# Input projection and gate: one 512-column matmul for both parts of the operand against the high weights, halves added on reading

## The chip, the core and the metric

The kernel runs on one core of one Trainium2 chip. A core has a matrix engine (PE, with its weight loads shown as PEld), a vector engine (DVE), a scalar engine (ACT), a general engine (POOL) and a queue engine (SP); each takes its instructions in order. PE writes to PSUM, which has eight banks; a bank holds 512 float32 numbers in each of the 128 partitions. The metric is the device time of one execution in microseconds (us): before the change the median of three runs is 992.47 us (992.36 to 992.50).

## The reference, cut to what matters

Two layers over 256 tokens of width 2048, all in float32:

```python
for i in range(DEPTH):                                  # DEPTH = 2
    u = _rmsnorm(h, norm_g[i]) @ w_in[i]                # input projection
    a_val, a_glu, a_z, q, k, v, b_z = jnp.split(u, offs, axis=-1)
    ya = _conformer_conv(a_val, a_glu, ...) * silu(a_z) # GLU, width-31 convolution, LayerNorm
    yb = _window_attention(q, k, v, bias_band, sink[i]) * silu(b_z)
    h = h + jnp.concatenate([ya, yb], axis=-1) @ w_out[i]   # output projection
    e = _rmsnorm(p[i] @ w_pe[i], pe_g[i])               # embedding
    h = h + e * sigmoid(h @ w_pg[i])                    # gate
return _rmsnorm(h, final_g)
```

## The kernel before, in words

**Products in parts.** Operands are kept transposed, channels in the partitions and the 256 tokens in the columns. To stay near float32 with a fast matmul type, each operand is the sum of a rounded high part and a low part (`hgh`, `hgl` for the normed input; `yah`/`yal`, `ybh`/`ybl` for the two branches; `h1h`, `h1l` for the residual), and so is each weight (`hi`, `lo`). A product of a 128x128 weight block with a 128x256 operand tile, called a *product* below, is three matmuls in `mm3` (lines 384 to 387): hi x high (L385), hi x low (L386), lo x high (L387). Each loads its own weights.

**Weight stream.** All weights come in 1 MB chunks in the order of use. Half a chunk (eight 128x128 blocks, a *half*) is split by `split` (L156 to L164): ACT casts it to `hi` (L161), then DVE subtracts to get `lo` (L164). `get(h)` is called at the start of the step that multiplies half h and splits up to half h+4 (there are five buffers, `NSPL`), so the parts run four halves ahead of PE.

**Stages of a layer.** The embedding `e`; then the input projection: eight convolution tiles `ag` (value and GLU column tile, a pair of output tiles in one PSUM bank), the keys `k`, the values `v` (other operand order, L580 to L582), four pairs each of `zb` and `q` in turn, and four pairs `za`; then the output projection `o`, and the gate `g`. A pair is four halves or 32 products. When a pair is complete, a consumer reads its bank: `glu` (ACT sigmoid L541, DVE multiply L542), casts and subtracts for the keys (L565, L567), SiLU on ACT for `zb` and `za` (L649, L669), scaling on ACT and DVE for `q` (L655, L656), sigmoid on ACT for `g` (L775).

**Side work.** After each step `pump` lets the side work go on: 2.6 to 3.3 taps of the convolution (L532, DVE; 240 taps a layer), and one step of attention, whose scores, transposes and values (`sc`, `pt`, `av`) each take PSUM banks for a while. At the end of the input projection DVE makes `ybl` (L713), which the output projection needs first.

**What sets the order.** PE, DVE and ACT carry out their instructions in the order in which the program text issues them, so an instruction that waits holds up everything behind it on its engine. The loads run on SP's queue and a few on POOL's. PSUM is one pool of eight banks, `ps`. The scratch tag `sq` has three buffers; one is held from the start by `oh` until the bias is prepared, during the `ag` stage.

Of the kernel before, what the change touches and what calls it, by code (L numbers as in the profile page):

```python
# [17 lines left out]
P = 128  # L18
# [42 lines left out]
# the convolution's column tiles, those that share the first operand's first half together  # L61
# [18 lines left out]
def weight_halves():  # L80
    """One layer's weights in the order of use: (matrix, columns, first k tile, k tiles)."""
# [39 lines left out]
# columns of the small per-channel parameters, one layer after the other  # L121
# [5 lines left out]
def trunk_kernel(ctx: ExitStack, tc: tile.TileContext, xT, pT, wst, par, gain, relb, sinkp, onehot, out):  # L127
# [4 lines left out]
    big = ctx.enter_context(tc.tile_pool(name="big", bufs=10))  # L132
# [4 lines left out]
    ps = ctx.enter_context(tc.tile_pool(name="ps", bufs=8, space=PSUM))  # L137
    dram = ctx.enter_context(tc.tile_pool(name="dram", bufs=1, space=DRAM))

    def bigt(name, dt=F32):  # L140
        return big.tile([P, 8, S], dt, tag="big", name=name)
# [15 lines left out]
    def split(h):  # L157
        raw = raws[h // 2][:, h % 2, :]
        hi = wspl.tile([P, HALF], F32R, tag="hi", name=f"hi{h}")
        lo = wspl.tile([P, HALF], F32R, tag="lo", name=f"lo{h}")  # L160
        nc.scalar.copy(hi, raw)  # L161
        spl[h] = (hi, lo)
        if h != 4:
            (nc.gpsimd if h in LOPOOL else nc.vector).tensor_sub(lo, raw, hi.bitcast(F32))  # L164

    def first_lo(x):
        """Half of the first half's low part."""
        s = slice(x * HALF // 2, (x + 1) * HALF // 2)
        nc.vector.tensor_sub(spl[4][1][:, s], raws[2][:, 0, s], spl[4][0][:, s].bitcast(F32))

    def ahead(h):
        """The parts of the halves up to h, and the loads that run ahead of them."""
# [9 lines left out]
    def get(h):  # L182
        """The two parts of half h."""
# [37 lines left out]
    def later(f, *args):  # L221
        """f(*args) with the next pump."""
# [11 lines left out]
    def finish(l):  # L234
        """What is left of the convolution and the attention."""
# [13 lines left out]
    # products of zeros while the first loads run, so that the PE's clock is up  # L249
    zeros = wk.tile([P, S], F32, name="zeros", tag="sq", bufs=3)  # L250
# [10 lines left out]
    def load_half(c, x, n=1):  # L261
        """Half of a chunk, in n parts."""
# [9 lines left out]
    h = [bigt(f"x{i}") for i in range(2)]  # L272
# [33 lines left out]
    oh = wk.tile([NUM_BUCKETS + 1, NREL], F32, name="oh", tag="sq", bufs=3)  # L306
# [5 lines left out]
    # keys, each head's parts twice, to meet the high and the low part of its queries  # L312
# [5 lines left out]
    def bias_prep():  # L318
# [3 lines left out]
        fs = wk.tile([NQ, NREL], F32, name="fs", tag="sq", bufs=3)  # L322
# [3 lines left out]
    def load_bias(i):  # L326
        """Minus the band's bias of tile i's two heads, [query, head, 3 * P - 1 - key of the band]."""
# [7 lines left out]
    def rstd_col(parts, dim, name, between=None):  # L335
        """(mean of squares + eps) ** -0.5 of each token, [P, 2]; parts: [P, S] partial sums."""
# [16 lines left out]
    def rstd_row(dg, name, tag="rb", copy=True):  # L353
        """The same in every row, [P, S]."""
# [16 lines left out]
    def square_acc(acc, src, first, eng=None):  # L371
        """acc += src * src, [P, 2, S]."""
# [3 lines left out]
        sq = wk.tile([P, 2, S], F32, name="sq", tag="sq", bufs=3)  # L376
# [7 lines left out]
    def mm3(o, wh, wl, xh, xl, start, stop):  # L384
        nc.tensor.matmul(o, wh, xh, start=start, stop=False, skip_group_check=True)  # L385
        nc.tensor.matmul(o, wh, xl, start=False, stop=False, skip_group_check=True)  # L386
        nc.tensor.matmul(o, wl, xh, start=False, stop=stop, skip_group_check=True)  # L387
# [4 lines left out]
    def step(o, X, start, stop):  # L392
        """The next half of the stream, times X, onto o."""
        steps([o], X, [start], stop)

    def steps(os, X, starts, stop):
        """The next halves of the stream (of the same rows), in turn by row tile."""
        parts = []
        for _ in os:
            name, _, k0, nk = HALVES[Cursor.h % NHALF]  # L400
            parts.append([a.rearrange("p (k c) -> p k c", k=nk) for a in get(Cursor.h)])
            Cursor.h += 1
        for kk in range(nk):
            k = k0 + kk
            for o, (hi, lo), start in zip(os, parts, starts):
                mm3(o, hi[:, kk, :], lo[:, kk, :], X[0][k // 8][:, k % 8, :], X[1][k // 8][:, k % 8, :],
                    start and kk == 0, stop and kk == nk - 1)
# [16 lines left out]
    for l in range(DEPTH):  # L424
        # ======== E: the layer's own embedding ========
        e = [bigt(f"e{l}_{i}") for i in range(2)]
        eacc = wk.tile([P, 2, S], F32, name="eacc", tag="hacc")
        # the first operand
        hg = ([], [])
        rbs, subs = [], []  # L430

        def operand(k, l=l, h=h, hg=hg):
            """Two tiles of the normed input, as parts."""
            i, kk = k // 8, k % 8
            if kk == 0:
                hg[0].append(bigt(f"hgh{l}_{i}", F32R))
                hg[1].append(bigt(f"hgl{l}_{i}", F32R))
# [458 lines left out]
```

## Time and profile before

| | |
|---|---|
| median of 3 runs | 992.47 us |
| the profiled execution: span | 992.5 us |
| PE busy | 972.7 us (98%), 7896 matmul records |
| DVE busy | 760.6 us (77%) |
| ACT busy | 545.6 us (55%) |
| POOL busy | 90.2 us (9%) |
| input projection, first layer | from 27.8 to 309.6 us |
| output projection, first layer | from 310.7 to 404.4 us |
| gate, first layer | from 404.4 to 496.7 us |
| second layer: input projection, gate | 512 to 790 us, 884.7 to 977 us |

The span of the profiled execution is its whole time; it stands at the median of the runs. Busy time says how long an engine had something in work, not that it was at its best pace: matmul records overlap, since the start of the next is what counts. In a timeline row the first number is the start, the second the length (of all, where several are merged), and what stands in brackets is the idle time of that engine just before, with the instruction that ended it.

### The profile page before, as it was taken

What the parts mean: (1) busy time and instruction counts of PE and PEld (TensorE: products, weight loads), DVE (VectorE), ACT (ScalarE), POOL (GpSimd) and SP (SyncE); (2) the same over time, 40 slices, a digit from 0 to 9 for tenths busy, and PEclk for the clock granted to TensorE, in tenths of its full rate; (3) what the DMA queues carried; (4) which work ended last, traced back from release to release, by engine and by line L of the source; (5) the groups of instructions that cost most, each with busy time, mean ns of one, the idle gap of its engine ahead of it and who ended that gap; (6) DMA issues with size and microseconds to landing.
All of it is one profiled execution on the core that took longest, in us unless ns stands there. A gap on an engine that the chain in (4) does not pass through costs nothing.

```text
span 992.5 us, 19137 instructions
## 1 busy us (share of the span) xinstructions
PE 972.7 (98%) x7896; PEld 952.6 (96%) x7896; DVE 760.6 (77%) x1284; ACT 545.6 (55%) x824; POOL 90.2 (9%) x91
## 2 busy tenths in 40 slices
PE   8999999999999999999999999999999999999994
PEld 6899999999999999999999999999999999999994
DVE  3899989987787666676658998988887867666653
ACT  4555454878774554444355444568777545445441
POOL 2113001001000000011103200000100000100110
PEclk9999999999999999999999999999999999999997
DMA  7665536555545466446556455455444435654522
GB/s 281 239 218 186 189 139 216 190 184 166 186 155 180 140 229 238 171 170 231 180 189 215 179 189 210 161 195 189 158 163 167 170 133 205 218 195 171 194 86 86
DMA packets 28888, 182.56 MB, mean 184 GB/s; under 512 B 3461, under 2 KB 4021, under 8 KB 8960
## 3 DMA queue, kind: packets, MB, share of 16 engines
q1 hardware_dynamic: 25200, 168.34, 47.2%
q0 software_dynamic: 3600, 12.99, 4.6%
q8 instruction: 62, 1.02, 0.4%
q14 instruction: 26, 0.21, 0.1%
HBM read 177.09 MB, written 4.23 MB: 183 GB/s over the span
## 4 chain that ended last, share of the span: by engine, by line
PE 94%; issue 3%; DVE 1%; POOL 1%; ACT 0%; POOLq 0%; DVEq 0%; ACTq 0%
PE o L385 6%; PE o L386 6%; PE o L387 6%; PE ag L386 6%; PE ag L385 6%; PE ag L387 6%; PE g L387 6%; PE g L386 6%; PE g L385 6%; PE za L385 3%; PE zb L385 3%; PE q L385 3%; PE zb L386 3%; PE q L386 3%; PE za L386 3%
## 5 line engine op out<-in xcount | busy, mean ns | idle before, releaser
L164 DVE TENSOR_TENSOR lo<-raw,hi 128x1024 fp32r<-128x1024 f32 x301 | 366.7, 1227 | 132.8 <-ACT hi L161 132.5
L161 ACT CAST hi<-raw 128x1024 fp32r<-128x1024 f32 x304 | 312.7, 1046 | 191.4 <-PE ag L386 46.0
L532 DVE SCALAR_TENSOR_TENSOR acc<-a,pars,acc 128x241 f32<-128x241 f32 (+11 forms) x480 | 217.8, 503 | 1.0
L386 PE MATMUL ag<-hgl,hi 128*128 128x256 f32 x512 | 145.1, 283 | 1.7 <-DVE hgl L445 1.7
L385 PE MATMUL ag<-hgh,hi 128*128 128x256 f32 x512 | 145.5, 284 | 0.0
L385 PE MATMUL g<-h1h,hi 128*128 128x256 f32 x512 | 144.9, 283 | 0.0
L386 PE MATMUL g<-h1l,hi 128*128 128x256 f32 x512 | 144.9, 283 | 0.0
L387 PE MATMUL g<-h1h,lo 128*128 128x256 f32 x512 | 144.9, 283 | 0.0
L387 PE MATMUL ag<-hgh,lo 128*128 128x256 f32 x512 | 144.9, 283 | 0.0
L386 PEld LDWEIGHTS ag<-hgl,hi 128*128 128x128 f32 x512 | 98.3, 192 | 2.2 <-DVE hgl L445 2.1
L385 PEld LDWEIGHTS ag<-hgh,hi 128*128 128x128 f32 x512 | 98.3, 192 | 1.2 <-ACT acc L525 0.8
L385 PEld LDWEIGHTS g<-h1h,hi 128*128 128x128 f32 x512 | 98.3, 192 | 0.0
L386 PEld LDWEIGHTS g<-h1l,hi 128*128 128x128 f32 x512 | 98.3, 192 | 0.0
L387 PEld LDWEIGHTS g<-h1h,lo 128*128 128x128 f32 x512 | 98.3, 192 | 0.0
L387 PEld LDWEIGHTS ag<-hgh,lo 128*128 128x128 f32 x512 | 98.3, 192 | 0.0
L385 PE MATMUL za<-hgh,hi 128*128 128x256 f32 x256 | 73.7, 288 | 0.0
L385 PE MATMUL o<-ybh,hi 128*128 128x256 f32 x256 | 73.3, 286 | 0.0
L385 PE MATMUL q<-hgh,hi 128*128 128x256 f32 x256 | 73.3, 286 | 0.0
L385 PE MATMUL zb<-hgh,hi 128*128 128x256 f32 x256 | 73.1, 286 | 0.0
L386 PE MATMUL o<-ybl,hi 128*128 128x256 f32 x256 | 72.5, 283 | 0.0
L385 PE MATMUL o<-yah,hi 128*128 128x256 f32 x256 | 72.4, 283 | 0.0
L386 PE MATMUL o<-yal,hi 128*128 128x256 f32 x256 | 72.4, 283 | 0.0
(214 smaller groups left out, 2277.9 us busy)
## 6 DMA issues: line engine op xcount, KB each, us to landing
raw<-in_wst SPq DMA_DIRECT2D x153, 1024.0 KB, 4.9
bias<-fscr POOLq DMA_DIRECT2D x16, 384.0 KB, 3.8
raw<-in_wst SPq DMA_DIRECT2D x5, 512.0 KB, 10.7
x<-in_xT SPq DMA_DIRECT2D x4, 512.0 KB, 11.4
hx<-in_xT POOLq DMA_DIRECT2D x8, 256.0 KB, 3.5
hscr<-e POOLq DMA_DIRECT2D x2, 1024.0 KB, 4.4
hx<-hscr POOLq DMA_DIRECT2D x8, 256.0 KB, 3.4
out_t<-og SPq DMA_DIRECT2D x7, 256.0 KB, 2.4
```

The source lines that it names most:

```text
L161: nc.scalar.copy(hi, raw)
L164: (nc.gpsimd if h in LOPOOL else nc.vector).tensor_sub(lo, raw, hi.bitcast(F32))
L385: nc.tensor.matmul(o, wh, xh, start=start, stop=False, skip_group_check=True)
L386: nc.tensor.matmul(o, wh, xl, start=False, stop=False, skip_group_check=True)
L387: nc.tensor.matmul(o, wl, xh, start=False, stop=stop, skip_group_check=True)
L532: nc.vector.scalar_tensor_tensor(acc[:, t, lo_:hi_], a[:, t, lo_ + s:hi_ + s], w(k), acc[:, t, lo_:hi_], ALU.mult, ALU.add)
```

## The change

The two parts of an operand now lie in one tile, `[P, 2, 8, S]`, so that high and low of a k tile can be read as one moving operand of 512 columns; the two parts of a weight half lie in one tile `w`. Where an output has a whole bank to itself, `mm3` issues two matmuls in place of three: the high weights against both parts at once (512 columns into the 512 of the bank), and the low weights against the high part onto the second half of the bank. An output tile then takes a bank instead of half a bank, and a pair takes two. On reading, `merge` adds the halves: ACT copies the second halves of the two banks to SBUF (`hl`, one buffer), DVE adds the first halves, and the consumers read the sum in SBUF. This is done for `ag`, `k`, `zb`, `q`, `za` and `g`; `o` and `v` keep three matmuls. PSUM is now two pools: `ps` with four single banks and `ps2` with two double ones. The tag `sq` goes from three buffers to two, the large tiles from ten to five of twice the size. Comments are dropped.

```diff
-    big = ctx.enter_context(tc.tile_pool(name="big", bufs=10))
+    big = ctx.enter_context(tc.tile_pool(name="big", bufs=5))
...
-    ps = ctx.enter_context(tc.tile_pool(name="ps", bufs=8, space=PSUM))
+    ps = ctx.enter_context(tc.tile_pool(name="ps", bufs=4, space=PSUM))
+    ps2 = ctx.enter_context(tc.tile_pool(name="ps2", bufs=2, space=PSUM))
...
+    def banks(name):
+        return ps2.tile([P, 2, 2, S], F32, tag="ps2", name=name)
...
-        sq = wk.tile([P, 2, S], F32, name="sq", tag="sq", bufs=3)
+        sq = wk.tile([P, 2, S], F32, name="sq", tag="sq", bufs=2)
...
-    def mm3(o, wh, wl, xh, xl, start, stop):
-        nc.tensor.matmul(o, wh, xh, start=start, stop=False, skip_group_check=True)
-        nc.tensor.matmul(o, wh, xl, start=False, stop=False, skip_group_check=True)
-        nc.tensor.matmul(o, wl, xh, start=False, stop=stop, skip_group_check=True)
+    def mm3(o, w, x, start, stop):
+        if len(o.shape) == 3:
+            nc.tensor.matmul(o, w[:, 0], x, start=start, stop=False, skip_group_check=True)
+            nc.tensor.matmul(o[:, 1], w[:, 1], x[:, 0], start=False, stop=stop, skip_group_check=True)
+            return
+        nc.tensor.matmul(o, w[:, 0], x[:, 0], start=start, stop=False, skip_group_check=True)
+        nc.tensor.matmul(o, w[:, 0], x[:, 1], start=False, stop=False, skip_group_check=True)
+        nc.tensor.matmul(o, w[:, 1], x[:, 0], start=False, stop=stop, skip_group_check=True)
+
+    def merge(b):
+        n = b.shape[1]
+        t = wk.tile([P, 2, S], F32, name="hl", tag="hl", bufs=1)[:, 0:n, :]
+        nc.scalar.copy(t, b[:, :, 1, :])
+        nc.vector.tensor_add(t, b[:, :, 0, :], t)
+        return t
...
     def pair(X, name):
-        b = bank(name)
+        b = banks(name)
         for x in range(2):
-            step(b[:, x, :], X, x == 0, False)
-            step(b[:, x, :], X, False, True)
-        return b
+            step(b[:, x], X, True, False)
+            step(b[:, x], X, False, True)
+        return merge(b)
...
         def glu(t, b):
+            b = merge(b)
             u = wk.tile([P, S], F32, name=f"u{l}_{t}", tag="sg")
             nc.scalar.activation(u, b[:, 1, :], AF.Sigmoid)
             nc.vector.tensor_mul(a[:, t, :], b[:, 0, :], u)
```

Where the prediction speaks of orders, these are the rows. On ACT, at the end of convolution tile 3 of the first layer (`sq<-e` are the embedding's squares, `u` the sigmoid of the GLU, `hi` or `w` the casts of the weights), before:

```order
L161 CAST hi_747<-raw_608 128x1024
L377 ACTIVATE sq<-e_0_130 128x512
L161 CAST hi_781<-raw_608 128x1024
L541 ACTIVATE u_3_812<-ag_3_676 128x256
L161 CAST hi_818<-raw_677 128x1024
```

and now:

```order
L170 CAST w_624<-raw_518 128x1024
L386 ACTIVATE sq<-e_132 128x512
L170 CAST w_649<-raw_518 128x1024
L408 COPY hl<-ag_3_571 128x512
L562 ACTIVATE u_3_674<-hl 128x256
L170 CAST w_680<-raw_572 128x1024
```

The copy of `merge` is new, and the sigmoid behind it now reads what DVE has added; the next cast stands behind both. On DVE at the same place, before:

```order
L532 SCALAR_TENSOR_TENSOR acc_266<-a_265,pars,acc_266 128x251
L532 SCALAR_TENSOR_TENSOR acc_266<-a_265,pars,acc_266 128x253
L532 SCALAR_TENSOR_TENSOR acc_266<-a_265,pars,acc_266 128x252
L542 TENSOR_TENSOR a_265<-ag_3_676,u_3_812 128x256
L164 TENSOR_TENSOR lo_819<-raw_677,hi_818 128x1024
```

and now:

```order
L552 SCALAR_TENSOR_TENSOR ac_261<-ac_261,pars 128x251
L552 SCALAR_TENSOR_TENSOR ac_261<-ac_261,pars 128x253
L552 SCALAR_TENSOR_TENSOR ac_261<-ac_261,pars 128x252
L409 TENSOR_TENSOR hl<-ag_3_571,hl 128x512
L563 TENSOR_TENSOR ac_261<-hl,u_3_674 128x256
L173 TENSOR_TENSOR w_680<-raw_572,w_680 128x1024
```

The add stands behind the taps of the last step, and ahead of the GLU's multiply and the next low part. For `zb` and `za` there is no multiply: the low part follows the add directly.

More of the change, by code (lines that the diff above doesn't have):

```diff
@@ L270, in load_x @@
         nc.sync.dma_start(h[k // 8][:, k % 8:k % 8 + 4, :], xT[:, k:k + 4, :])
-    h = [bigt(f"x{i}") for i in range(2)]
+    h = halves(bigt("x"))
     pf = load_p(0)
@@ L545, in trunk_kernel @@
         for ts in FIRST_TILES:
-            bs = [bank(f"ag{l}_{t}") for t in ts]
+            bs = [banks(f"ag{l}_{t}") for t in ts]
             for n in range(2):
@@ L716, in trunk_kernel @@
         side.append(lgen)
-        Y = ([ya[0], yb[0]], [ya[1], yb[1]])
-        ob = [bank(f"o{l}_{j}") for j in range(NB_FIRST // 2)]
+        Y = [ya, yb]
+        ob = []
+        for j in range(2):
+            b = banks(f"o{l}_{j}")
+            ob += [b[:, 0], b[:, 1]]
+        ob += [bank(f"o{l}_{j}") for j in range(4, NB_FIRST // 2)]
         for j in range(NB_FIRST):
@@ L804, in trunk_kernel @@
         for j in range(KT - 2, KT):
-            b = bank(f"g{l}_{j}")[:, 0:1, :]
-            step(b[:, 0, :], h1, True, False)
-            step(b[:, 0, :], h1, False, True)
-            gate(j, b)
+            b = banks(f"g{l}_{j}")[:, 0:1]
+            step(b[:, 0], h1, True, False)
+            step(b[:, 0], h1, False, True)
+            gate(j, merge(b))
         drain()
```

89 lines of the change are left out of this document (41 added, 48 removed).

## The prediction

> **What bounds the kernel now.** I read the page first, then the chain of waits, then stretches of the input projection, then single rows there.
>
> ```profile
> PE 972.7 (98%) x7896; PEld 952.6 (96%) x7896; DVE 760.6 (77%) x1284; ACT 545.6 (55%) x824; POOL 90.2 (9%) x91
> PE 94%; issue 3%; DVE 1%; POOL 1%; ACT 0%; POOLq 0%; DVEq 0%; ACTq 0%
> ```
>
> PE carries 94% of the chain, and nothing else holds it for long: the bound is the pace of its matmuls. That pace is read from starts, not lengths. From the timeline of PE and its loads, and the chain:
>
> ```profile
> 850.25 0.28 PE L385 MATMUL o<-yah,hi 128*128 128x256 f32 x1
> 850.25 0.19 PEld L386 LDWEIGHTS o<-yal,hi 128*128 128x128 f32 x1
> 850.37 0.28 PE L386 MATMUL o<-yal,hi 128*128 128x256 f32 x1
> 496.68 5.18 PE e L462 x24
> L385 PE MATMUL g<-h1h,hi 128*128 128x256 f32 x512 | 144.9, 283 | 0.0
> ```
>
> A 256-column matmul follows the one before by 120 ns, so a product of three takes 360 ns. The load for the next matmul begins with the matmul it hides under. The float32 matmuls of the embedding, whose two records stand for four passes over 256 columns, take 5.18/24 = 216 ns a record, 108 per 256 columns: longer streams seem to carry less surplus than 120 ns, and the surplus looks like the weight load.
>
> But the 77% of DVE is a mean. These are stretches of the two input projections, between a low part that DVE makes at the end of a tile and another (first layer: end of tile 1, end of the first `q` pair, start of `ybl`; second layer alike), and the two gates; after PE and PEld comes DVE:
>
> ```profile
> 54.72:174.76 120.04, 120.04 (x994) 119.00 (x993) 114.40 (x192) 58.85 (x77) 18.59 (x14) 1.00 0.55 192
> 174.76:308.99 134.23, 134.23 (x1113) 128.92 (x1113) 112.97 (x250) 98.71 (x184) 9.11 (x11) 1.00 0.52 177
> 536.61:655.20 118.59, 118.59 (x989) 118.54 (x989) 112.34 (x191) 57.20 (x74) 14.34 (x9) 1.00 0.53 187
> 655.20:789.20 134.00, 134.00 (x1111) 128.71 (x1111) 112.41 (x250) 98.44 (x184) 7.10 (x8) 1.00 0.48 169
> 404.40:496.70 92.30, 92.30 (x771) 92.30 (x770) 61.11 (x75) 41.21 (x48) 8.32 (x7) 1.00 0.55 193
> 884.70:977.00 92.30, 92.30 (x773) 92.30 (x771) 56.95 (x73) 45.33 (x61) 7.75 (x6) 1.00 0.39 138
> ```
>
> In the first half of a projection DVE works 95% of the time, and there it runs behind PE. The sigmoid on ACT marks the end of a tile on PE, the next row of DVE the low part that follows:
>
> ```profile
> 66.03 0.38 ACT L541 ACTIVATE u<-ag 128x256 f32<-128x256 f32 x1 [1.95 <-PE ag L387]
> 67.39 1.23 DVE L164 TENSOR_TENSOR lo<-raw,hi 128x1024 fp32r<-128x1024 f32 x1
> 77.56 0.38 ACT L541 ACTIVATE u<-ag 128x256 f32<-128x256 f32 x1 [1.95 <-PE ag L387]
> 79.45 1.21 DVE L164 TENSOR_TENSOR lo<-raw,hi 128x1024 fp32r<-128x1024 f32 x1
> ```
>
> DVE needs 12.06 us for a tile that PE does in 11.53. So PE and DVE are level in that half; in the gates DVE has a third to spare.
>
> **The change part by part.** *PE, the pace.* Removed: one of three matmuls and loads in each of 1856 products (`ag`, `g` 512 each; `zb`, `q`, `za` 256 each; `k` 64). What 512 columns of this type cost is not in the trace. From below: two streams without surplus, 216 + 108 = 324 ns. From above: 120 ns for every 256 columns, 360, no gain. I take 216 + 120 = 336: the low weights load under the long matmul, the next high weights under the short one, which stays load-bound. That is 24 ns a product, 0.77 us a pair, 44.5 us in all if nothing else binds.
>
> The Trainium skill ("TensorE: Matmul & The Clock Gate", Back-to-back issue gap) gives N/2.4 + 2.5 ns between isolated warm matmuls, 109 for 256 columns and 216 for 512. The embedding's rows agree with the second, the 120 ns disagree with the first; by the rule alone only 2.5 ns a product would be won, 1.3 us in the gates, and the sum below would come to 1008 (the rival without gain in pace, to within 2 us).
>
> *Gates.* DVE and ACT have room for the merges there: the added copy, add and repeated wait take some 2 us of a pair of 10.8, and the parts run four halves ahead. So 512 products x 24 ns = **-12.3 us**, between -18.4 and 0.
>
> *Input projections.* Here each `merge` adds an ACT copy and a DVE add, and, as the orders show, a loop: DVE adds, ACT reads the sum, ACT then casts the next weights, DVE then makes their low part. Before, ACT read PSUM as soon as PE was done, and its casts were ready when a late DVE came to them. Now a late DVE finds ACT blocked behind its own add, and waits out the loop. The prices:
>
> ```profile
> L741 DVE TENSOR_TENSOR hx<-o,hx 128x512 f32<-128x512 f32 x16 | 11.0, 691 | 7.5 <-PE o L387 7.5
> 529.20 0.38 ACT L541 ACTIVATE u<-ag 128x256 f32<-128x256 f32 x1 [3.13 <-PE ag L387]
> 529.61 0.42 DVE L542 TENSOR_TENSOR a<-ag,u 128x256 f32<-128x256 f32 x1 [2.64 <-ACT u L541]
> 530.54 2.36 DVE L164 TENSOR_TENSOR lo<-raw,hi 128x1024 fp32r<-128x1024 f32 x2 [0.51 <-ACT hi L161]
> 212.53 0.60 ACT L649 ACTIVATE zb<-zb 128x512 f32<-128x512 f32 x1
> 213.02 1.98 ACT L161 CAST hi<-raw 128x1024 fp32r<-128x1024 f32 x2
> 172.34 0.69 DVE L656 SCALAR_TENSOR_TENSOR qq<-q,qq 64x512 fp32r<-64x512 f32 x1
> 173.68 0.69 DVE L656 SCALAR_TENSOR_TENSOR qq<-q,qq 64x512 fp32r<-64x512 f32 x1 [0.66 <-ACT qq L655]
> 174.76 1.23 DVE L164 TENSOR_TENSOR lo<-raw,hi 128x1024 fp32r<-128x1024 f32 x1 [0.39 <-ACT hi L161]
> 616.45 1.50 ACT L565 CAST keys0h<-k 64x256 fp32r<-64x256 f32 x4 [1.95 <-PE k L387]
> 314.31 1.28 DVE L685 TENSOR_TENSOR acc<-acc,mu 128x512 f32<-128x512 f32 x2
> ```
>
> The add is like `hx<-o,hx`: 0.69, and some 0.6 of DVE's time where the next follows closely (the last row, 1.28 - 0.69). An `ag` tile: 0.72 for the add and the way to ACT, then 1.34 from sigmoid to low part (529.20 to 530.54) = 2.06, of which the multiply's 0.34 was DVE's work before: **+1.7**. `zb` and `za`: 0.72 + 0.49 (212.53 to 213.02) + 1.07 for one cast = **+2.3**. `q`: 0.72, two scalings 0.5 apart, 0.5 more to the cast, 1.07 = 2.8, less 1.37 that DVE works of 172.34 to 174.76: **+1.4**. `k`: 0.72 and two of the four casts of 1.50: **+1.5**.
>
> The first stretch holds six `ag` tiles, `k`, one `zb`, one `q`: 6 x 1.7 + 1.5 + 2.3 + 1.4 = 15.4. DVE then needs 114.40 + 15.4 = 129.8 us, where PE took 120.04 and would need 113.1 at 336 ns. In the second layer 112.34 + 15.4 = 127.7 against 118.59. The lead of four halves, some 10 us, only shifts this: it is used up within the stretch, PE then waits for low parts, and at the end the lead is paid back, since `ybl` stands behind all of it on DVE. The second stretch holds three `zb` and three `za` loops, three `q`, and a last add: 6 x 2.3 + 3 x 1.4 + 0.6 = 18.6. DVE needs 112.97 + 18.6 = 131.6 against 134.23, and 131.0 against 134.00; PE alone would need 126.5. So DVE sets both stretches: +9.8 - 2.7 + 9.1 - 3.0 = **+13.2 us** over the two layers, in place of the -32 that PE would give. Ahead of 54.72, tiles 0 and 1 save 64 x 24 ns = 1.5 on PE, and the first loops give 1.4 back.
>
> *Small terms.* POOL's step in the embedding's norm stops DVE for 0.83 in each layer whatever its lag: **+1.7**. At the start, `sq` has two buffers, one held by `oh`, so that squares and adds no longer overlap:
>
> ```profile
> 130.72 0.48 DVE L350 TENSOR_SCALAR re0dg<-ident,re0col 128x128 f32<-128x128 f32 x2 [0.83 <-POOL re0col L345]
> 16.38 1.15 ACT L377 ACTIVATE sq<-x 128x512 f32<-128x512 f32 x2 [0.94 <-DMA x<-in_xT]
> 18.57 0.63 ACT L470 ACTIVATE sq<-x 128x512 f32<-128x512 f32 x1
> 17.05 2.29 DVE L378 TENSOR_TENSOR hacc<-hacc,sq 128x512 f32<-128x512 f32 x3 [1.08 <-ACT sq L377]
> 19.98 0.28 PE L340 MATMUL rh0c<-ones,fold 128*128 128x1 f32 x2
> 977.23 0.38 ACT L775 ACTIVATE sg<-g 128x256 f32<-128x256 f32 x1 [3.54 <-PE g L387]
> ```
>
> From 16.6 on, three times 0.63 + 0.69 with 0.06 between, a copy's tail and the last square: it ends near 21.4 where PE went on at 19.98: **+1.5**. At the end the last sigmoid waits for a copy and an add of 256 columns, like 0.38 and 0.43: **+0.9**. Four PSUM banks in place of eight for embedding and attention cost nothing as long as each is read within a step.
>
> *Sum.* -12.3 + 13.2 + 1.7 + 1.5 + 0.9 = +5.0 on a span of 992.5, which is the median: **997.5 us**; 990 to 1006 with 2 us of doubt on each stretch of the projections and half the bounds of the gate.
>
> **The rivals.**
>
> ```profile
> L164 DVE TENSOR_TENSOR lo<-raw,hi 128x1024 fp32r<-128x1024 f32 x301 | 366.7, 1227 | 132.8 <-ACT hi L161 132.5
> 203.10 0.28 PE L604 MATMUL sc<-keys0h,qq 128*128 128x256 f32 x1
> 206.93 1.03 PE L631 MATMUL pt<-ident,s 128*128 128x128 f32 x8
> 213.64 1.08 PE L641 MATMUL av<-ptt,v 128*64 128x256 f32 x8
> 217.62 0.28 PE L604 MATMUL sc<-keys0h,qq 128*128 128x256 f32 x1
> ```
>
> *DVE pays the adds alone*, since the loops fall into time in which it is idle anyway: the first stretches need 114.4 + 9 x 0.6 = 119.8 and 117.7, as before, and the second ones follow PE, about -8 each: 992.5 - 16 - 12.3 + 4.1 = 968. For it speaks that DVE waits 132.5 us for casts over the run; against it, that only 5.6 of the first stretch's 120.04 are idle. *PE sets everything*: 992.5 - 44.5 + 2.4 = 950; against it, DVE would have to do 119.8 us of work in 113.1. *No gain in pace* (360 ns, if the moving data cost 120 ns for every 256 columns): 997.5 + 12.3 = 1010; the embedding's 108 speaks against it, though of another type. *Attention ties the engines together*, on the slower side: scores, transposes and values of one tile of heads take five banks between 203.10 and 217.62, and four are there. PE then waits for a bank that a late DVE has yet to read, and DVE for PE. It decides once DVE's lag passes a step of 2.7 us; at some 1 us for each of the 16 tiles of heads, half a step's doubt, it gives 1013.
>
> **How the numbers follow.** The forecast 0.50 (0.40 of it slower by over 0.2%, which is about what a measurement here can tell, 0.10 within), adds alone 0.15, PE alone 0.10, no pace 0.10, attention 0.15. That is faster 0.25, same 0.10, slower 0.65. The range takes in the second, fourth and fifth and stops above the third: 962 to 1014.
>
> **What would show it.** Wide matmuls 216 ns ahead of the next start, and gates of about 86 us, show the pace; gates of 92 would refute it. In the projections PE idle before low-part matmuls, released by DVE, with DVE waiting about 0.5 to 1 us at each merge for ACT, and stretches of 128 to 132 us, show the loop. Projections near 265 us in place of 282 and 278 would refute it, and with it the sign.

## The result, and the profile after the change

| | before | after |
|---|---|---|
| median | 992.49 us | 1022.38 us (1019.21 to 1023.36) |
| ratio | | 1.0297 (95% interval 1.0280 to 1.0314) |
| profiled execution: span | 992.5 us | 1021.0 us |
| mean granted clock of PE (1 is full speed) | 0.992 | 0.981 |

The change makes the kernel 3% slower. The forecast was 997.5 us with a range of 962 to 1014: the sign was right, the size was not. The page of the changed kernel, busy times and the chain:

```profile
PE 974.1 (95%) x6040; PEld 859.4 (84%) x6040; DVE 797.8 (78%) x1344; ACT 573.1 (56%) x884; POOL 89.0 (9%) x91
...
PE 73%; DVE 20%; ACT 3%; issue 2%; DMA 1%; POOL 0%; SPq 0%; POOLq 0%; ACTq 0%; DVEq 0%
```

PE carries 73% of the chain in place of 94%; DVE, 1% before, now carries 20%. The stages of the profiled executions, by the first start of each on PE (the second gate to the end of its last matmul):

| stage | before | after | difference |
|---|---|---|---|
| ahead of `ag`, first layer | 27.8 | 28.9 | +1.1 |
| input projections, first and second layer | 282.9, 279.6 | 294.2, 291.3 | +11.4, +11.8 |
| output projections | 93.7, 93.7 | 97.0, 97.0 | +3.3, +3.3 |
| gates | 92.2, 92.3 | 90.5, 90.6 | -1.7, -1.7 |
| second embedding | 15.0 | 15.8 | +0.7 |
| behind the last gate | 15.4 | 15.7 | +0.3 |

That is +28.5, the difference of the two spans. The first and the last row are the least certain: in the kept traces of all the kernels below `ag` starts anywhere between 25.6 and 29.1 us. The stretches of the forecast (first and second stretch of each projection, between the same low parts on DVE, and the gates), after the change; columns as before, from a view of busy time by stretch:

```profile
57.93:189.74 131.81, 121.37 (x696) 105.15 (x695) 120.97 (x201) 61.84 (x86) 17.97 (x14) 0.97 0.49 174
189.74:323.24 133.50, 133.50 (x805) 113.08 (x804) 118.52 (x261) 103.62 (x194) 9.11 (x11) 0.99 0.51 176
420.20:510.60 90.40, 90.40 (x514) 78.35 (x513) 65.23 (x82) 45.42 (x56) 8.33 (x7) 1.00 0.53 193
554.32:683.28 128.96, 117.87 (x685) 102.49 (x685) 118.15 (x198) 59.93 (x83) 13.76 (x9) 0.98 0.49 172
683.28:817.79 134.51, 134.51 (x805) 114.06 (x805) 118.51 (x260) 103.80 (x194) 7.09 (x8) 0.98 0.49 167
```

In the first stretch PE is busy 121.37 of 131.81 us, where it had no idle time at all; DVE works 6.6 us more than before (120.97 against 114.40) and stands idle for 10.8, before for 5.6. In the second stretches it is the other way round: PE has no idle time (133.50 of 133.50, 134.51 of 134.51) and DVE stands for 15 and 16 us. Two things are new.

**ACT waits for DVE at every merge.** From the timelines of ACT, DVE and PE at the end of convolution tile 5:

```profile
89.88 0.58 ACT L408 COPY hl<-ag 128x512 f32<-128x512 f32 x1
...
98.23 0.68 DVE L409 TENSOR_TENSOR hl<-ag,hl 128x512 f32<-128x512 f32 x1
...
98.94 0.42 ACT L562 ACTIVATE u<-hl 128x256 f32<-128x256 f32 x1 [8.49 <-DVE hl L409]
...
99.39 0.42 DVE L563 TENSOR_TENSOR ac<-hl,u 128x256 f32<-128x256 f32 x1 [0.48 <-ACT u L562]
100.33 1.23 DVE L173 TENSOR_TENSOR w<-raw,w 128x1024 fp32r<-128x1024 f32 x1 [0.52 <-ACT w L170]
...
101.61 0.39 PE L398 MATMUL ag<-hg,w 128*128 128x256 f32 x1 [0.69 <-DVE w L173]
```

ACT has copied the second halves at 90.5. DVE, behind by then, comes to the add at 98.23; for 8.49 us ACT does nothing, though the casts of the next weights stand ready behind the sigmoid. When DVE has added, it waits itself, 0.48 for the sigmoid and 0.52 for the cast, and PE waits for the low part.

**PE stops long enough to lose its clock.** The longest waits of PE after the change (engine, line, what it waited for; us in all, times, longest):

```profile
PE ag L398 <- DVE w L173: 6.3, 10, 1.4
PE sc L622 <- DVE qq L674: 6.3, 3, 4.3
PE re0b L365 <- DVE re0dg L359: 4.4, 1, 4.4
PE re1b L365 <- DVE re1dg L359: 3.8, 1, 3.8
PE o L400 <- DVE hx L761: 3.5, 4, 0.9
...
PE o L401 <- DVE yb L730: 1.5, 4, 0.4
```

Only the first is the wait that was forecast. At the scores `sc` and at the embedding's norm `re0b` a PE instruction of the side work needs a result that a late DVE has not made, and everything queued behind it on PE stops too. PE alone, microsecond by microsecond around the stop at `re0b` and behind the one at `sc` (stretch, length, PE busy, matmuls, granted clock, share of the DMA engines, GB/s):

```profile
139.00:140.00 1.00, 0.64 (x4) 1.00 0.61 254
...
142.00:143.00 1.00, 0.00 (x0) 0.80 0.00 0
...
145.00:146.00 1.00, 1.00 (x6) 0.50 1.03 434
...
149.00:150.00 1.00, 1.00 (x9) 0.79 0.94 131
...
187.00:188.00 1.00, 0.00 (x0) 1.00 0.78 295
...
190.00:191.00 1.00, 1.00 (x7) 0.69 0.00 0
```

At `re0b` PE stands from 139.6 on; after 3 us the granted clock falls to half and stays there until 149.4, some 5 us into the work that follows. This happens four times ahead of the end of the last gate (from 142.6, 190.4, 613.6 and 681.9 us, for 6.8, 3.4, 3.4 and 6.8 us), some 20 us at half clock in all. The Trainium skill ("TensorE: Matmul & The Clock Gate", The HAM clock gate) has the clock fall to half after an idle window of about 3.4 us. This trace is near that figure, but a whole window was not needed: the falls came after some 3.0, 2.0, 3.7 and 3.9 us of idle time in the 4 us before, and at 190.4 PE had been at work again since 189.5.

### The profile page after: what moved, and what is told of

It reads as the page before. It is cut to its first block, busy times and chain, and to the rows that moved or that the text cites. A ratio compares the mean times of both kernels' runs of the same rounds, so it can differ in the third digit from the quotient of the medians.

```text
span 1021.0 us, 15399 instructions
## 1 busy us (share of the span) xinstructions
PE 974.1 (95%) x6040; PEld 859.4 (84%) x6040; DVE 797.8 (78%) x1344; ACT 573.1 (56%) x884; POOL 89.0 (9%) x91
## 4 chain that ended last, share of the span: by engine, by line
PE 73%; DVE 20%; ACT 3%; issue 2%; DMA 1%; POOL 0%; SPq 0%; POOLq 0%; ACTq 0%; DVEq 0%
PE g L397 11%; DVE ac L552 8%; DVE w L173 7%; PE o L400 6%; PE o L401 6%; PE za L397 6%; PE o L402 6%; PE g L398 6%; PE q L397 5%; PE zb L397 5%; PE ag L397 4%; PE za L398 3%; PE q L398 2%; PE zb L398 2%; PE ag L398 2%
## 5 line engine op out<-in xcount | busy, mean ns | idle before, releaser
L173 DVE TENSOR_TENSOR w<-raw,w 128x1024 fp32r<-128x1024 f32 x301 | 366.7, 1228 | 127.1 <-ACT w L170 126.6
L170 ACT CAST w<-raw 128x1024 fp32r<-128x1024 f32 x304 | 307.1, 1044 | 76.6 <-PE o L402 24.1
L552 DVE SCALAR_TENSOR_TENSOR ac<-ac,pars 128x241 f32<-128x241 f32 (+11 forms) x480 | 217.8, 503 | 1.0
L397 PE MATMUL ag<-hg,w 128*128 128x512 f32 x512 | 182.6, 400 | 2.0 <-DVE hg L466 2.0
L397 PE MATMUL g<-h,w 128*128 128x512 f32 x512 | 181.0, 399 | 0.0
L398 PE MATMUL ag<-hg,w 128*128 128x256 f32 x512 | 145.0, 283 | 6.3 <-DVE w L173 6.3
L397 PEld LDWEIGHTS ag<-hg,w 128*128 128x128 f32 x512 | 96.7, 189 | 26.4 <-DVE hg L466 2.7
L397 PEld LDWEIGHTS g<-h,w 128*128 128x128 f32 x512 | 96.2, 188 | 24.0
L398 PEld LDWEIGHTS ag<-hg,w 128*128 128x128 f32 x512 | 97.2, 190 | 9.6 <-DVE w L173 9.5
L398 PEld LDWEIGHTS g<-h,w 128*128 128x128 f32 x512 | 96.7, 189 | 0.0
L400 PE MATMUL o<-ya,w 128*128 128x256 f32 x256 | 72.7, 284 | 3.5 <-DVE hx L761 3.5
L401 PE MATMUL o<-yb,w 128*128 128x256 f32 x256 | 72.8, 285 | 1.5 <-DVE yb L730 1.5
L400 PE MATMUL o<-yb,w 128*128 128x256 f32 x256 | 73.2, 286 | 0.0
L401 PE MATMUL o<-ya,w 128*128 128x256 f32 x256 | 72.4, 283 | 0.0
L402 PE MATMUL o<-ya,w 128*128 128x256 f32 x256 | 72.4, 283 | 0.0
L402 PE MATMUL o<-yb,w 128*128 128x256 f32 x256 | 72.4, 283 | 0.0
```

What stands on the lines that cost most here:

```text
L397: nc.tensor.matmul(o, w[:, 0], x, start=start, stop=False, skip_group_check=True)
L398: nc.tensor.matmul(o[:, 1], w[:, 1], x[:, 0], start=False, stop=stop, skip_group_check=True)
L400: nc.tensor.matmul(o, w[:, 0], x[:, 0], start=start, stop=False, skip_group_check=True)
L401: nc.tensor.matmul(o, w[:, 0], x[:, 1], start=False, stop=False, skip_group_check=True)
L402: nc.tensor.matmul(o, w[:, 1], x[:, 0], start=False, stop=stop, skip_group_check=True)
L552: nc.vector.scalar_tensor_tensor(acc[:, t, lo_:hi_], a[:, t, lo_ + s:hi_ + s], w(k), acc[:, t, lo_:hi_], ALU.mult, ALU.add)
```

## Experiments

All times are medians of runs beside the kernel before on the same chip (992.3 to 992.8 there).

**Pace alone.** Series of matmuls with a new weight block each, with nothing beside them (N is 64):

```diff
+    o = bank("w512")
+    for i in range(N):
+        mm(o, wv[:, 0, i % 8], xa[:, :, i % 8], i, N)
```

> A kernel that leaves out the whole computation: series of 64 matmuls of one form each, every one with another 128x128 weight block than the one before, on a chip that does nothing else meanwhile. In the changed kernel a 512-column matmul takes 236 ns and a 256-column one 118. If the surplus over 108 ns is the weight load, as the prediction had it, the series of 512 columns takes about 216 to 228 ns a matmul, and 384, 128 and 64 columns take some 120 to 170, 120 and 120. If it is the rate of the moving data for this type, time goes with the columns: 236, 177, 59 and 30 ns or whatever the load leaves. If it is the gap between the two halves of the moving operand, 512 columns side by side take 216 and 512 with a gap 236. If it is the work of the other engines or of the DMAs, all of them are near 108 per 256 columns here. If it is the data, the series of zeros is faster than the one of the same shape.

The rows of some series: 512 columns side by side, zeros, three matmuls a product, 384 columns, 128 and 64 columns, and two series of a 16-bit type, bf16 (durations least, median, largest in ns, then first and last start):

```profile
L167 PE MATMUL w512c<-xc,w x64: 389/389/389, 45.6 to 59.9; 128*128 128x512 f32 x64
...
L167 PE MATMUL zero<-xz,w x64: 389/389/397, 159.4 to 173.7; 128*128 128x512 f32 x64
...
L167 PE MATMUL three<-xa,w x192: 278/283/283, 136.4 to 159.3; 128*128 128x256 f32 x192
...
L167 PE MATMUL n<-xc,w x64: 333/334/346, 60.1 to 71.1; 128*128 128x384 f32 x64
...
L167 PE MATMUL n<-xa,w x61: 272/275/277, 71.5 to 78.2; 128*128 128x128 f32 x61
...
L167 PE MATMUL n<-xa,w x16: 277/277/279, 78.4 to 80.1; 128*128 128x64 f32 x16
...
L167 PE MATMUL b<-xb,wb x64: 272/273/273, 187.7 to 194.6; 128*128 128x256 bf16 x64
...
L167 PE MATMUL b<-xb,wb x63: 379/379/379, 194.9 to 208.3; 128*128 128x512 bf16 x63
```

512 columns take 14.3/63 = 227 ns, 384 take 174 (60.12 to 71.06 us over 63), 256 take 22.9/191 = 120. Between 256 and 512 columns time grows by 107 ns, as the 108 of the embedding's passes, and 13 ns stay on each matmul. So the surplus belongs to the matmul, not to the columns, and neither the gap nor the data plays a part. Nor is it a weight load that a long matmul hides, as the prediction had it: 128 and 64 columns follow one another by some 112 ns alike, so whatever sets the pace there needs less than the 120 ns of 256 columns, and 384 and 512 columns keep the surplus all the same. It belongs to this type: bf16 with a new block each time takes 109 and 216 ns. A product of two is then 227 + 120 = 347 ns (348 in its own series): 13 ns less than three, not 24. In the changed kernel it is not even that. The gate, from PE's timeline:

```profile
449.87 0.40 PE L397 MATMUL g<-h,w 128*128 128x512 f32 x1
450.10 0.28 PE L398 MATMUL g<-h,w 128*128 128x256 f32 x1
450.22 0.40 PE L397 MATMUL g<-h,w 128*128 128x512 f32 x1
450.46 0.28 PE L398 MATMUL g<-h,w 128*128 128x256 f32 x1
450.58 0.40 PE L397 MATMUL g<-h,w 128*128 128x512 f32 x1
```

A product starts every 0.35 or 0.36 us; over the gate the mean is 353.3 ns, 6.7 ns less than three matmuls: 236 ns behind a wide one, alone 230, and 117 behind a narrow one in both. Two more kernels looked for what takes the other 6 ns.

> A kernel that leaves out the whole computation: series of 64 products of a 512-column and a 256-column matmul. Alone such a product took 347 ns, in the changed kernel 353.3, in every microsecond of the gate. base: as alone; turn: two halves of a double bank in turn; tiles: weights and operands from two tiles in turn; engines: with casts on ACT and subtractions on DVE at the same time; dma: with 1 MB loads at the same time; last: alone. If the other engines or the loads cost the 6.5 ns, their series takes 353 and the rest 347; if it is the bank or the tiles, theirs does.

> A kernel that leaves out the whole computation: series of 64 products of a 512-column and a 256-column matmul. Alone they take 347 ns a product (230 + 117), in the changed kernel 353.3 (237 + 117). lolo: operand and weights at low addresses of SBUF; xhigh, whigh, both: operand, weights or both some 100 KB higher; data: other values; sixteen: another accumulation and other tiles every 16 or 8 products. If an address makes the 6.6 ns, one of xhigh, whigh and both takes 353; if the values do, data does; if none, it stays open what does.

```profile
L181 PE MATMUL base<-xa,w x64: 391/391/391, 40.9 to 62.8; 128*128 128x512 f32 x64
...
L181 PE MATMUL turn<-xa,w x64: 391/391/391, 63.1 to 85.0; 128*128 128x512 f32 x64
...
L181 PE MATMUL engines<-xa,w x64: 391/391/391, 107.5 to 129.3; 128*128 128x512 f32 x64
...
L181 PE MATMUL dma<-xa,w x64: 391/391/391, 129.7 to 151.5; 128*128 128x512 f32 x64
```

All four are 346 to 348 ns a product (21.8 or 21.9 over 63), and so are all series of the second at full clock, with other addresses, values and accumulations. (While `engines` ran, ACT and DVE were busy for 15 and 16 of 22 us; while `dma` ran, the DMA engines for 71%.) What costs the 6 ns in place stays open.

**Three matmuls again, merge kept.**

```diff
-            nc.tensor.matmul(o, w[:, 0], x, start=start, stop=False, ...)
+            nc.tensor.matmul(o[:, 0], w[:, 0], x[:, 0], start=start, stop=False, ...)
+            nc.tensor.matmul(o[:, 1], w[:, 0], x[:, 1], start=False, stop=False, ...)
```

> The changed kernel with its merges, but with three 256-column matmuls a product again, each onto its half of the bank. The theory that DVE sets the projections (and that the wide matmul gave only some 6 us there and 4 in the gates) says: the gates go back to 92.3 each (+3.6 together), the rest moves little, 1024 to 1028 us. The rival, that PE still sets the pace in the projections in between its waits, says 1856 products x 6.5 ns = 12 us more, 1034.

Measured 1029.97 us, ratio 1.0381 (1.0366 to 1.0396): between the two. The wide matmul is worth 7.6 us in the changed kernel, of which the gates have 3.4; of the 9.0 us that it could win in the projections (1344 x 6.7 ns), about half arrives. That would fit the second stretches, where PE has no idle time (640 products, 4.3 us).

**No merge.**

```diff
...
-        nc.scalar.copy(t, b[:, :, 1, :])
-        nc.vector.tensor_add(t, b[:, :, 0, :], t)
-        return t
+        return b[:, :, 0, :]
```

> The changed kernel without the copy and the add on reading: the consumers read the first halves of the banks alone, so that the products with the low parts are left out of the result, while PE does all its matmuls. If the merge and the loop that it ties is the cause, the projections go back to PE's pace: 992.5 - 1856 x 6.5 ns + 1.5 at the start + about 4 in the output projections = 986. If the four single and two double PSUM banks are the cause, it stays above 1005. If the forecast's pace of 336 ns held where nothing waits, it would be near 953.

Measured 983.88 us, ratio 0.9918 (0.9899 to 0.9936). All the loss and more, 38.5 us, comes with the merge; pools, banks and layouts cost little: 95.9 in place of 93.7 in each output projection and 0.7 in the second embedding.

**The casts ahead of the merge.** In `merge`, the casts and low parts that the next step asks for (`parts_for`) are issued first; then the same in `ag`, `k`, `zb` and `q` alone.

```diff
     def merge(b):
+        if Cursor.h % NHALF >= 4:
+            parts_for(Cursor.h)
         n = b.shape[1]
```

> The changed kernel with one thing moved: the casts of the next weight halves, and the low parts behind them, are issued ahead of the merge's copy and add, so that no cast waits for the add. The loop theory: the stretches of the projections then cost the adds and copies alone, some 121 us for the first ones, and the second ones follow PE; PE's long stops at the embedding's norm and at the scores go with the lag that makes them: 986 to 995 us. If the work of DVE itself is the cause and not the loop, 1012 to 1020. If the stops at the embedding's norm and the scores, and the half clock behind them, are a cause of their own, they stay and it is about 1005.

> The changed kernel with the casts ahead of the merge in the stages ag, k, zb and q alone, not in za and the gates. With the casts ahead everywhere the first stretches had been some 7 and 6 us shorter, and the gates and output projections as much longer. If that is right, this keeps the first and not the second: 1022 - 12 = 1010. If what is won in the first stretches is only lost again in the zb and q stages (DVE's work decides over both), 1016 to 1020.

Everywhere: 1020.62 us, ratio 1.0282 (1.0255 to 1.0309). By its time that speaks for DVE's work as the cause, but it is the sum of two opposite effects: the start and the projections up to `za` won some 12 us, and `za`, the output projections and the first gate lost as much. Ahead of a copy of the gate now stand casts whose data have not come; from the timeline of ACT, 6.17 us late:

```profile
500.16 1.99 ACT L170 CAST w<-raw 128x1024 fp32r<-128x1024 f32 x2 [6.17 <-DMA raw<-in_wst]
502.06 0.58 ACT L414 COPY hl<-g 128x512 f32<-128x512 f32 x1
```

In the four stages alone it is 1009.63 us, 1.0173 (1.0159 to 1.0186), as expected. So the cast behind the add costs about 13 of the 38 us; 25 stay.

**Three small edits at separate places**, and the same together with the first form of the casts ahead.

```diff
             dg = rstd_col([es], D, f"re{l}")
-            yield from wait(2)
+            yield from wait(5)
...
-    oh = wk.tile([NUM_BUCKETS + 1, NREL], F32, name="oh", tag="sq", bufs=2)
+    oh = wk.tile([NUM_BUCKETS + 1, NREL], F32, name="oh", tag="s", bufs=4)
...
-            if j % 2:
+            if j % 4 == 3 and j < 8:
+                resid(j - 3, ob[j // 2 - 1])
+                resid(j - 1, ob[j // 2])
+            elif j % 2 and j >= 8:
                 resid(j - 1, ob[j // 2])
```

> Three edits at separate places, read from their own stages: the embedding norm's broadcast on PE three steps later; zeros, one-hot and bias scratch in another tag, so that the squares at the start have both buffers; and in the output projection the residual of each first tile of a double bank delayed until its partner is done. The start goes back by 1 to 1.5 us; the output projections lose the two stops of 0.9 each and go from 97 to 95. The stops of 4.4 and 3.8 us at the embedding's norm go, and the half clock behind them; if they are a cause of their own, that is worth 4.4 + 3.8 and some 2.5 for each half-clock stretch: with the rest 1022 - 1.5 - 3.6 - 13 = 1004. If DVE sets the stretch, PE only waits for low parts elsewhere: 1022 - 5 = 1017.

> The casts ahead of the merge, with the three edits at separate places (embedding norm three steps later, the start's scratch in another tag, residuals of a double bank delayed). If the loop and these small terms are all that the change cost beside its gain: 1856 x 6.5 ns less than before plus 0.9 at the end and about 2.5 left in the output projections, 984. If the adds and copies cost time by themselves, 990 or more.

The edits alone: 1016.13 us, 1.0238 (1.0223 to 1.0254); together with the casts ahead 1014.06, 1.0218 (1.0203 to 1.0233), far from 984. The edits come out as was said for a DVE that sets the stretch (1017): each output projection goes from 97.0 to 94.8, together 4.4 of the 6.2 us won. The start is 1.5 shorter in this trace, but that lies within what it varies by without this edit. The stop at the embedding's norm is gone from its place, but PE now stops at `zb` and the clock falls there (at 153.5 in place of 142.6 us); the time at half clock is 20 us as before. In these stretches, which DVE sets, the stop was not a cost of its own: what PE did not lose there it lost at the next place.

**The merge's work with nobody behind it.** The copy and the add are done, the consumers read the banks; in the second form the add leaves the banks alone.

```diff
         nc.vector.tensor_add(t, b[:, :, 0, :], t)
-        return t
+        return b[:, :, 0, :]
...
-        nc.vector.tensor_add(t, b[:, :, 0, :], t)
-        return t
+        nc.vector.tensor_add(t, t, t)
+        return b[:, :, 0, :]
```

> The changed kernel where the copy and the add of every merge are still done, but nobody waits for them: the consumers read the first halves of the banks (the low parts are left out of the result). Without copy and add it took 984. If the work of the merges on DVE and ACT is what costs, 1000 to 1010 here. If it is the dependence (copy, add, consumer, cast, low part one behind the other), 984 to 990.

> The changed kernel where the merge's work is done beside the consumers: ACT copies the second halves to a scratch buffer, DVE adds that buffer to itself, and the consumers read the first halves of the banks (the low parts are left out of the result). In the kernel of the label work the sigmoid and the scalings still waited for the add, since it read the same bank; here nothing on ACT waits for it but the copy of the next merge. Without copy and add: 984. If the dependence (sigmoid, cast and low part behind the add) is all the cost, 984 to 988. If DVE's added work counts where DVE sets the pace (eight or nine adds of 0.69 us in each first stretch, 12 us in all), 996 and more.

The first gave 1028.06 us, 1.0357 (1.0343 to 1.0371), but it had not taken the dependence away. Its waits of ACT:

```profile
ACT u L562 <- DVE hl L409: 85.9, 15, 8.5
```

In the changed kernel it is the same:

```profile
ACT u L562 <- DVE hl L409: 85.8, 15, 8.5
```

The sigmoid no longer reads the sum, yet it is held until DVE has read the same bank: the program sets an order between two engines' readings of one bank. The Trainium skill ("PSUM — Partial Sum Buffer", its passage on bank collisions) says that the compiler's scheduler sets such an order between instructions of different engines on one bank and the same 32 partitions, readings included; this run agrees. The second form, where the add reads SBUF alone and nothing but the next copy waits for it, gave 993.27 us, 1.0004 (0.9994 to 1.0014), above the 984 to 988 for a cost of waiting alone and below the 996 for work that counts in full. So the work of the merges costs some 9 us over no merge, and that others wait for it costs 29.

**The add on POOL**, with the casts ahead in four stages and the three edits; ACT copies both halves.

```diff
+            nc.scalar.copy(t, b)
+            nc.gpsimd.tensor_add(t[:, :, 0, :], t[:, :, 0, :], t[:, :, 1, :])
```

> The casts ahead of the merge in ag, k, zb and q, the three edits at separate places, and in these stages the add on POOL instead of DVE: ACT copies both halves of the banks, POOL adds them in SBUF. Without the POOL step this stands at about 1009.6 - 5.6 = 1004. If DVE's work is what is left of the cost, the stretches lose the adds (5 to 6 us each): 990 to 994, or 984 if PE sets the pace then. If the longer way from bank to consumer (some 2 to 3 us in place of 1.3) counts, 1004 or more.

Measured 1007.87 us, 1.0161 (1.0146 to 1.0177). DVE is rid of these adds and nothing is won over the 1004 that were estimated without this step. Now ACT waits for POOL, whose add takes 1648 ns on the average, and its casts wait for loads, 48.0 us in all against 2.2 with the casts ahead in four stages alone; which of the two eats the gain was not separated:

```profile
ACT w L170 <- DMA raw<-in_wst: 48.0, 20, 5.5
ACT u L572 <- POOL hl L416: 34.1, 16, 4.5
```

**The consumers two steps later.** Copy and add stay where they are; sigmoid and multiply, key casts, SiLU of `zb` and the scalings of `q` are issued two steps later, with casts of weights between.

```diff
         def glu(t, b):
             b = merge(b)
+            def use():
                 u = wk.tile(...)
                 nc.scalar.activation(u, b[:, 1, :], AF.Sigmoid)
                 nc.vector.tensor_mul(a[:, t, :], b[:, 0, :], u)
                 conv_q.append(conv(t))
+            after_steps(1, use)
```

> The changed kernel with one thing moved: in ag, k, zb and q the consumers of the merged sum (sigmoid and multiply, key casts, SiLU, scalings) are issued two steps after the merge, with two casts of weights between; copy and add stay where they are. If ACT's blocking behind the add is the dependence that costs, it falls to about what the work alone made, 993 (990 to 998). If the length of the way from bank to consumer matters, or DVE's order, it stays above 1005.

Measured 994.38 us, ratio 1.0016 (1.0007 to 1.0025): 28 of the 29 us are back, with every copy, add and wide matmul in place. At the end of the first `q` pair, DVE of the changed kernel, then of this one:

```profile
186.64 0.68 DVE L409 TENSOR_TENSOR hl<-q,hl 128x512 f32<-128x512 f32 x1
188.01 1.40 DVE L674 SCALAR_TENSOR_TENSOR qq<-hl,qq 64x512 fp32r<-64x512 f32 x2 [0.69 <-ACT qq L673]
189.74 1.22 DVE L173 TENSOR_TENSOR w<-raw,w 128x1024 fp32r<-128x1024 f32 x1 [0.32 <-ACT w L170]
```

```profile
173.76 0.68 DVE L415 TENSOR_TENSOR hl<-q,hl 128x512 f32<-128x512 f32 x1
174.36 1.22 DVE L173 TENSOR_TENSOR w<-raw,w 128x1024 fp32r<-128x1024 f32 x1
...
177.89 1.40 DVE L687 SCALAR_TENSOR_TENSOR qq<-hl,qq 64x512 fp32r<-64x512 f32 x2
```

and a stretch of it, columns as above:

```profile
57.00:189.00 132.00, 131.38 (x780) 115.67 (x779) 129.96 (x227) 68.54 (x94) 21.48 (x14) 1.00 0.54 190
```

The low part follows the add at once, DVE waits for nothing there, and from 57 to 189 us it works 129.96 of 132.00 us; no half clock is left in the projections.

**Versions that keep a gain.** The wide matmul in the gates alone; in the gates and `za`; and everywhere, with late consumers, the three small edits and three matmuls for the gates' last single tiles. In the first two, `wide` takes two single banks out of one pool of eight and merges them.

```diff
-            b = pair(hg, f"za{l}_{t}")
+            b = wide(hg, f"za{l}_{t}", "u", 3)
```

> The wide matmul and the merge in the gates alone, single banks out of one pool of eight everywhere, three buffers of the squares, the merged halves in a scratch buffer of the attention. With 353.5 ns a product the gates take 90.4 in place of 92.3 each: 992.5 - 3.7 + 0.9 at the end = 989.7. With the forecast's pace of 336 ns it would be 981. If the merge costs in the gates too, no better than 992.

> The wide matmul in the gates (their last single tile with three narrow ones) and in za, eight single banks, all else as before the change. In the gates and in za DVE works 66% and 79% of the time, so the merges should fit: 992.5 - 2 x 1.8 - 2 x 0.8 = 987.3, nothing lost at the end. If the merges cost in za (attention's banks or DVE), no better than the gates alone, 990.3.

> The same with the three edits at separate places (start's scratch in another tag, embedding norm three steps later, residuals of a double bank delayed) and three narrow matmuls for the last single tile of the gates. With the edits' 5.6 us and 0.9 at the end less than the run before it: some 987, under the 990.0 of the wide matmul in gates and za alone. If the stretch is bound by DVE's work, the edits in it win nothing and only the output projections' 3.5 go: 989 to 990.

Gates alone: 990.33 us, 0.9977 (0.9968 to 0.9986); the gates take 90.5 each. With `za`: 989.99, 0.9971 (0.9959 to 0.9983), not the 987.3 expected: `za` is 1.0 us shorter in each layer, and the output projection behind it 1.2 longer. There PE now waits 1.6 us in all for `yb`, before for nothing; that the last merge, which stands ahead of these low parts on DVE, is the reason was not tried by itself. Everywhere with late consumers: 987.49 us, 0.9954 (0.9940 to 0.9967), as expected. It beats both kernels, by 0.5% and 3.4%.

## Why the prediction was wrong, and where it was right

**The bound: right.** PE's pace, and DVE level with it in the first half of a projection, is what decided. With nobody waiting for the merges the kernel stays at 993: their work on DVE and ACT alone, some 9 us, eats the gain in pace.

**The pace: mis-sized.** This is the first step that failed, "512 products x 24 ns = -12.3". It took the surplus for a weight load that a long matmul hides. The surplus stays on each matmul, and leaving one out wins 13 ns alone and 6.7 in place. In the kernel the next start comes 236 ns behind a wide matmul, not 216, and the first gate stands at 90.5, between the 86 that were to show the pace and the 92 that were to refute it: the two gates won 3.4 us, not 12.3, +8.9 of the miss. The rule of the Trainium skill that was weighed there and set aside ("TensorE: Matmul & The Clock Gate", Back-to-back issue gap: only 2.5 ns a product to be won) was nearer in its result, though not in its pace: 227 and 120 ns are not its 216 and 109. The bf16 series agrees with it. The embedding's rows misled: its passes carry no such surplus.

**The loop: right in kind, and near in price.** Adds, sigmoid, cast and low part in a ring on two engines was the mechanism, and the waits stand where they were to be seen. With POOL's 0.83 the first stretches were forecast at 130.6 and 128.5 us and came out at 131.8 and 129.0. The prediction priced one turn of the loop on DVE's side. The runs show the side of ACT too: it stands up to 8.5 us behind a late DVE, and so do the casts in its queue. Moving only the next cast won 13 us, moving the consumers 28.

**"So DVE sets both stretches": wrong for the second ones.** The term "+13.2", with POOL's +1.7 14.9, measured 11.8 - 0.7 + 10.4 + 0.5 = 22.0, and 5.5 of the 7.1 between them lie in the second stretches. DVE was to set them at 131.6 and 131.0 us, with PE done in 126.5 at 336 ns a product. But PE took 133.5 and 134.5 there without idle time, and DVE had 15 and 16 us to spare. An estimate from the rows: 320 products x 6.7 ns less than before make 132.1 and 131.9, and PE's 3.4 and 5.4 us at half clock within them add half their length, 133.8 and 134.6. So the pace failed here a second time, and half clock came on top.

**The lead "is used up within the stretch, PE then waits for low parts": half right.** PE's longest stops were not before low parts but before the side work's own instructions on PE (`sc`, `re0b`), which wait for a late DVE. That a stop then costs clock was not foreseen. In the first stretches it was not a cost of its own, since without the stop the time came out elsewhere; what the half clock of the second stretches costs was not tried by itself.

**"Four PSUM banks ... cost nothing": right for attention, wrong for the output projection.** Without the merge the projections run at PE's pace with the same banks (277.1 us for the first), so the rival on attention falls. But two outputs `o` share a double bank, and the second pass onto one waits until the other's residual has been read (`o L400 <- DVE hx`, four times 0.9). That is a term that the sum put at nothing. Without the merge each output projection is 2.2 longer than before, with the last merge ahead of `yb` 3.3, +6.7 in the two; delaying residuals gave back 2.2 in each.

**Small terms.** Start +1.1 against +1.5 and end +0.3 against +0.9 lie within what the traces vary by; the second embedding's +0.7, there in each kernel with the two pools, was not foreseen. The miss on the span: 8.9 (gates) + 8.2 (projections, 23.1 against the forecast's 13.2 and 1.7) + 6.7 + 0.7 - 0.4 - 0.6 = 23.5, which with the forecast's 5.0 is the 28.5 measured.

**The rivals.** *Adds alone* and *PE sets everything* were the faster ones; the runs that come nearest to them gave 993 and 984, not 968 and 950, in the main because both built on 336 ns (1856 products at 353 take 32 us more). *Attention* was nearest in number (1013), but not by its mechanism: PE's waits at the scores are for an operand that DVE makes late (`sc <- DVE qq`), not for a bank. *No gain in pace* (1010) was nearest where the prediction failed: nearly three quarters of the gain did not come.

## What to carry to other kernels

In this kernel, an operation that joins two engines did not cost its own length where one of them was late: it made the other as late, with all that was queued behind it. Look at what stands in the queue behind a new wait, and put work that is already possible between the producer and its consumer; here that was worth 28 us, where the joining work itself cost some 9. Two outputs in one allocation, and two readers of one bank, waited for each other here even where they shared no data. And a surplus per instruction should be measured at the new size before it is put into a sum.

## What the runs showed of the hardware that was not expected

A 256-column matmul of this type follows the one before by 120 ns, 384 by 174, 512 by 227: a fixed 13 ns over 107 ns for 256 columns. Below that, 128 and 64 columns both take some 112. In bf16 256 and 512 columns take 109 and 216. In the full kernel a pair of 512 and 256 columns takes 353.3 ns; alone it took 346 to 348 with every bank, address, value and neighbour that was tried.

The granted clock falls without any idle time too. In the first pace kernel PE ran series of 128 and then 64 columns, back to back, from 71.2 us on (columns as above):

```profile
79.00:80.00 1.00, 1.00 (x12) 1.00 0.00 0
80.00:81.00 1.00, 1.00 (x8) 0.61 0.00 0
...
92.00:93.00 1.00, 1.00 (x5) 0.50 0.00 0
...
94.00:95.00 1.00, 1.00 (x8) 1.00 0.00 0
```

The clock went to half within the microsecond from 80 and came back between 93 and 94, over 3 us after the 512-column matmuls of the next series had begun at 90.2. It looks as if short matmuls do not count as full work; that was not tried by itself.
